# Block sums of weights in a two-layer diffusion kernel: from VectorE to accumulating loads, with turned signs in the activations

## The chip, the core and the metric

The kernel runs on one core of a Trainium2 chip. The core has a matmul engine (TensorE, PE in the profile, with its weight loads as PEld), VectorE (DVE), ScalarE (ACT), GpSimd (POOL) and SyncE (SP); the last one only issues transfers here. Transfers run on 16 DMA engines that all issuing engines share. The metric is the device time of one execution in microseconds (us); lower is better. The median of three runs of the kernel before is 872.34 us (872.25 to 872.8).

## The reference

One sequence of 512 latent tokens and 256 context tokens of width 1024 goes through two layers, and a normalisation ends it. Layer 0 is a retention mixer, layer 1 a gated MLP that mixes tokens in chunks of 128. The change lies in layer 1:

```python
def gmlp_chunk_mixer(h, w_in, vnorm_g, w_s, b_s, w_out):
    u = h @ w_in[:, :GM_WIDTH]                       # GM_WIDTH = 2048
    v = (h @ w_in[:, GM_WIDTH:2 * GM_WIDTH]).astype(F32)
    z = h @ w_in[:, 2 * GM_WIDTH:]
    v = v - jnp.mean(v, axis=-1, keepdims=True)
    v = v * lax.rsqrt(jnp.mean(v * v, axis=-1, keepdims=True) + NORM_EPS) * vnorm_g.astype(F32)
    ...
    mixed = jnp.einsum('gij,bnjgc->bnigc', w_s.astype(F32), vg) + b_s.astype(F32).T[:, :, None]
    y = u * mixed.reshape(b, l, w).astype(u.dtype)
    return (y * jax.nn.silu(z)) @ w_out
```

All of it is float32.

## The kernel before

**Seven products instead of eight.** A projection h @ w is cut into 2 x 2 blocks: token halves and feature halves of h, row halves and column halves of w. A "quad" is four weight blocks 11, 12, 21, 22 of 512 KB each (two transfers of 256 KB). Instead of eight block products the kernel computes seven, in the way of Strassen and Winograd, from sums of weight blocks and sums of activation blocks. The table `USES` names the weights' side: B11, B21 and B22 are plain blocks, T1 = 12 - 11, T2 = 22 - T1, T3 = 22 - 12, T4 = 21 - T2. `WITH` names the activations' side: A11, A12, A22 plain, S1 to S4 sums. The products are added up in PSUM banks and, through a `snap` (a copy of a bank) and a `plus` (bank and snap combined), into the four output blocks.

**Split operands.** Each float32 operand is cut into a high and a low part in the fast float32 format (`split`, line 133: ScalarE casts the high part, shown as CAST hl<-raw; VectorE subtracts, shown as TENSOR_TENSOR hl<-raw,hl), and each product is three matmuls (`mm3`). A product of a quad is 24 matmuls of 256 columns.

**The stream of weights.** One object, `Stream`, holds the order of all products (`items`) and of all loads (`loads`). `get` hands the next product its split weights and splits two products ahead (`upto`), into four `hl` buffers. `pump` issues the next load from SyncE as soon as one of the raw slots is free (for layer 1's u/z quads and the output projection: seven slots of 512 KB, w0 to w6); a slot comes free when the last product that needs its block is split (`drop`). `sum` forms T1 to T4 on VectorE in place in the raw slots (shown as TENSOR_TENSOR raw<-raw): T1 into 11's slot, T2 into the same, T3 into 12's, T4 into 21's.

**Layer 1.** First come four quads of v (`v1`, products in pairs, `PAIRED`), whose results are spilled to HBM as vt by GpSimd; then eight quads of u and z (`("u", i)`, products in the order `SINGLE` = B11, T1, T2, B21, T3, B22, T4), each with one block row of u and one of z; beside each quad the chunk mixing (`spatial`, `norm_vt`, `gate_f`). After quads 2, 4 and 6 a quarter of the output projection follows (`out1`, quarter 2 in two halves around quad 7), and the last quarter at the end. The operands A11 to S4 of layer 1 are made once, by `half_sum`, `first_half` and `second_half`, and serve both the v quads and the u/z quads.

**What sets the order.** Instructions of TensorE, ScalarE, VectorE and SyncE go through one helper (`Queue`), so the profile shows them all at its line 54 and is read by tile names; GpSimd's transfers show at the line that issues them (142 for spills, 1400 for the residual). Each engine runs its own instructions in order. A scheduler places them from the text, with orders pinned for TensorE, ScalarE and VectorE in places; transfers of SyncE and of GpSimd are issued in the order that the scheduler gives, each after its waits, and a transfer that waits holds up all behind it on the same issuing engine. The output projection already has eight accumulating loads from GpSimd (o<-x, the residual).

Of the kernel before, what the change touches and what calls it, by code (L numbers as in the profile page):

```python
# [67 lines left out]
def hybrid_kernel(ctx, tc, xT_d, cT_d, cv_d, sv_d, rows_d, ada0_d, adag_d, w_d, rope_d, dec_d, ws_d, id_d, out_d):  # L68
# [83 lines left out]
    PAIRED = ("B11", "B21", "T1", "T2", "B22", "T3", "T4")  # L152
    SINGLE = ("B11", "T1", "T2", "B21", "T3", "B22", "T4")

    class Stream:
# [18 lines left out]

        def load(self, key, slots, stage, parts):
            self.loads.append((key, slots, stage, parts))

# [4 lines left out]
        def pump(self):  # L182
            while self.sent < (self.cap or len(self.loads)):
                key, slots, stage, parts = self.loads[self.sent]
                ok = [s for s in self.free if s in slots]
                if stage > self.stage or not ok:
                    return
                self.free.remove(ok[0])
                r = st([P, 1024], ok[0], name="raw")
                for dst, src in parts:  # L190
                    load(dst(r), src)
                self.raws[key] = r
                self.left[key] = [ok[0], sum(it[0] == key[0] and key[1] in it[2] for it in self.items)]
                self.sent += 1

        def upto(self, n, late=None):

            while self.done < min(n, self.limit or len(self.items)):
# [24 lines left out]
        def sum(self, n):  # L223
# [3 lines left out]
            q, name, uses, at, place = self.items[n]  # L227
            if name[0] not in ("T", "gated") or any((q, u) not in self.raws for u in uses):
                return
# [7 lines left out]
            else:  # L237
                dve.tensor_tensor(r, raw(uses[0]), raw(uses[1]), ALU.subtract)

# [89 lines left out]
    A = {}  # L329
# [44 lines left out]
    class Product:  # L374

        def __init__(self, product, done, side=None, z="tm"):
            self.product, self.done, self.side, self.z_tag, self.s = product, done, side, z, {}

        def snap(self, key, bank):
            t = self.s[key] = t2("snap")
            act.copy(t, bank)

        def plus(self, key, bank, name):
            t = self.s.pop(key)
            dve.tensor_tensor(t, bank, t, ALU.add)
            self.done(name, t)
# [479 lines left out]
    def background():  # L868
        for i in range(4):
# [324 lines left out]
    def half_sum(hf, m):  # L1194
        if hf == 1:
# [65 lines left out]
    def second_half():  # L1261
# [362 lines left out]
```

## Time and profile before

| | |
|---|---|
| median of three runs | 872.34 us |
| profiled execution | 872.05 us, span 870.0 us |
| TensorE busy | 860.7 us, 99% |
| VectorE busy | 713.8 us, 82% |
| ScalarE busy | 457.8 us, 53% |
| GpSimd busy | 58.4 us, 7% |
| moved by DMA | 153.81 MB, mean 177 GB/s |

The span is the time from the first to the last instruction; the profiled execution's own time is 2.05 us longer. A group of the profile reads: engine, operation, output<-input, shape, count, then busy time in us and the mean of one in ns, then the idle time of that engine before these instructions, with what ended most of it. In the 40 slices of the span each digit is a busy share in tenths. A DMA queue's row gives packets, megabytes and the time its packets took as a share of 16 engines; q1 is SyncE's queue, q0 GpSimd's. A row of the windows gives the stretch, its length, each engine's busy time with the number of instructions, and last the granted TensorE clock, the DMA share and GB/s.

### The profile page before, as it was taken

The page shows a single profiled execution, that of the slowest core. Times are in us where ns is not written, and L with a number is a line of the kernel's source. Part 1 is how long each engine was busy: PE and PEld are TensorE (multiplying, and loading weights), DVE is VectorE, ACT ScalarE, POOL GpSimd, SP SyncE. Part 2 cuts the span into 40 slices and gives each one's busy share as a digit, 9 for nine tenths or more (in the row PEclk, how much of TensorE's full clock was granted, in tenths as well). Part 3 has the DMA queues.
Part 4 walks back from the last instruction along what each step waited for, and adds up shares of the span by engine and source line. Part 5 has one row for each costly group of instructions (what it writes and reads, how often), then busy time and mean ns, then how long its engine had stood idle before and what let it go on. Part 6 is the DMA issues. An engine that isn't in the chain of part 4 may idle for free.

```text
span 870.0 us, 17009 instructions
## 1 busy us (share of the span) xinstructions
PE 860.7 (99%) x6906; PEld 824.3 (95%) x6906; DVE 713.8 (82%) x998; ACT 457.8 (53%) x709; POOL 58.4 (7%) x96
## 2 busy tenths in 40 slices
PE   8999999999999999999999999999999999999997
PEld 7899999999999999999989899999999899899986
DVE  4799978699789777888677679999899488688995
ACT  4475644434545346637363549744666456256434
POOL 0001201102102011000000002011000000000110
PEclk9999999999999999999999999999999999999999
DMA  9943967557667458747164602535435036035523
GB/s 349 406 155 105 310 220 262 162 186 234 203 226 244 144 195 324 267 159 249 67 213 151 198 21 108 198 133 206 135 122 194 25 122 201 18 122 170 122 41 105
DMA packets 75774, 153.81 MB, mean 177 GB/s; under 512 B 7728, under 2 KB 34864, under 8 KB 75696
## 3 DMA queue, kind: packets, MB, share of 16 engines
q1 hardware_dynamic: 67392, 128.40, 44.1%
q0 software_dynamic: 7872, 24.12, 8.1%
q8 instruction: 54, 0.88, 0.4%
q10 hardware_dynamic: 432, 0.20, 0.1%
q14 instruction: 24, 0.20, 0.1%
HBM read 128.58 MB, written 24.12 MB: 176 GB/s over the span
## 4 chain that ended last, share of the span: by engine, by line
PE 96%; DMA 2%; ACT 0%; DVE 0%; SPq 0%; issue 0%; DVEq 0%; ACTq 0%
PE pst L54 96%; DMA raw<-in_w_dram 1%; DMA ada_w<-in_ada_dram 1%; DVE o L54 0%; ACT junk L54 0%; SPq L54 0%; ACT fss L54 0%; ACT o L54 0%; DVE fss L54 0%; ACT hl L54 0%; DVEq L1620 0%; ACTq L54 0%
## 5 line engine op out<-in xcount | busy, mean ns | idle before, releaser
L54 DVE TENSOR_TENSOR hl<-raw,hl 128x1024 fp32r<-128x1024 f32 (+2 forms) x197 | 234.8, 1197 | 69.1 <-ACT hl L54 68.8
L54 ACT CAST hl<-raw 128x1024 fp32r<-128x1024 f32 (+2 forms) x197 | 203.0, 1034 | 138.2 <-PE pst L54 57.6
L54 PE MATMUL pst<-hl,oS 128*128 128x256 f32 x1152 | 133.2, 276 | 0.0
L54 PE MATMUL pst<-oS,hl 128*128 128x256 f32 x1104 | 132.6, 277 | 0.1
L54 PEld LDWEIGHTS pst<-hl,oS 128*128 128x128 f32 x1152 | 131.8, 188 | 0.4 <-issue 0.4
L54 PEld LDWEIGHTS pst<-oS,hl 128*128 128x128 f32 x1104 | 128.2, 188 | 1.0 <-ACT oS L54 0.6
L54 PE MATMUL pst<-oA,hl 128*128 128x256 f32 x936 | 116.6, 279 | 0.9 <-DVE hl L54 0.5
L54 PEld LDWEIGHTS pst<-oA,hl 128*128 128x128 f32 x936 | 110.6, 188 | 3.2 <-ACT hl L54 1.0
L54 DVE TENSOR_TENSOR raw<-raw 128x1024 f32<-128x1024 f32 x92 | 111.9, 1218 | 0.8
L54 ACT COPY snap<-pst 128x512 f32<-128x512 f32 x92 | 53.6, 584 | 90.5 <-PE pst L54 90.4
L54 PE MATMUL pst<-hl,oA 128*128 128x256 f32 x768 | 92.7, 277 | 0.0
L54 PE MATMUL pst<-og,hl 128*128 128x256 f32 x768 | 91.1, 278 | 0.0
L54 PEld LDWEIGHTS pst<-hl,oA 128*128 128x128 f32 x768 | 89.5, 188 | 0.2
L54 PEld LDWEIGHTS pst<-og,hl 128*128 128x128 f32 x768 | 89.2, 188 | 0.3
L54 PE MATMUL pst<-v,ph 128*128 128x512 f32 x192 | 59.8, 393 | 0.0
L54 PE MATMUL pst<-hl,ya 128*128 128x512 f32 (+1 forms) x246 | 59.1, 386 | 0.0
L54 PEld LDWEIGHTS pst<-hl,ya 128*128 128x128 f32 x246 | 45.3, 188 | 9.5
L54 DVE TENSOR_TENSOR snap<-pst,snap 128x512 f32<-128x512 f32 x69 | 47.1, 683 | 5.1 <-PE pst L54 5.1
L54 PE MATMUL pst<-hl,hc 128*128 128x256 f32 x384 | 46.1, 276 | 0.0
L54 PEld LDWEIGHTS pst<-hl,hc 128*128 128x128 f32 x384 | 44.7, 188 | 0.0
L54 ACT CAST ph<-pf 128x512 fp32r<-128x512 f32 x24 | 14.8, 618 | 55.3 <-DVE pf L54 54.8
L54 PEld LDWEIGHTS pst<-v,ph 128*128 128x128 f32 x192 | 36.1, 188 | 7.1
(186 smaller groups left out, 1022.7 us busy)
## 6 DMA issues: line engine op xcount, KB each, us to landing
raw<-in_w_dram SPq DMA_DIRECT2D x224, 256.0 KB, 4.0
bg<-in_adag_dram SPq DMA_DIRECT2D x32, 512.0 KB, 4.2
ada_w<-in_ada_dram SPq DMA_DIRECT2D x16, 512.0 KB, 9.0
raw<-in_w_dram SPq DMA_DIRECT2D x16, 512.0 KB, 4.4
bg<-in_dec_dram SPq DMA_DIRECT2D x12, 512.0 KB, 4.3
v<-snap POOLq DMA_DIRECT2D x16, 256.0 KB, 5.6
z<-snap POOLq DMA_DIRECT2D x16, 256.0 KB, 5.0
v<-v SPq DMA_DIRECT2D x8, 512.0 KB, 4.3
```

What stands on the lines that cost most here:

```text
L54: made = op(*args, **kw)
```

## The change

The u/z quads no longer have their sums formed on VectorE. The signs of the recipe are turned so that all weight sums are plain additions: with T1 = 11 + 12, T2 = 22 + 12 + 11 and T3 = 22 + 12, a tile can be loaded with one block, and the others are added to it in SBUF by accumulating loads that GpSimd issues (`accum_op=ALU.add`). The table `SUMMED` says which. Six tiles are loaded for a quad in place of four. T4 is T2's tile with block 21 added on top after T2 has been split, so T2's slot stays taken until T4 is split. Per quad that is 12 plain transfers of 256 KB in place of 8, and 10 accumulating ones; over eight quads 32 and 80 more. The v quads keep VectorE's sums, with T1 now an addition.

The turned signs are put into the activations, once for both sets of quads: S1, S2 and S4 come from differences where there were sums (and the reverse), S2 with a scale of -1 in its split; and in `Product`, with `turned`, the snaps of T1 and T2 are taken with a scale of -1 and `plus` subtracts the bank.

```diff
+    SUMMED = {"B11": ("11",), "T1": ("11", "12"), "T2": ("22", "12", "11"), "B21": ("21",), "T3": ("22", "12"), "B22": ("22",)}
...
+        def loaded(self, q, slots, stage):
+
+            for name in SINGLE:
+                if name == "T4":
+                    self.items.append((q, name, ("T2",), "T2", None))
+                    continue
+                self.items.append((q, name, (name,), name, None))
+                first, *more = SUMMED[name]
+                self.load((q, name), slots, stage, parts_of(q, first), [parts_of(q, u) for u in more])
+
+        def add(self, r, parts):
+            for dst, src in parts:
+                nc.gpsimd.dma_start(dst(r), src, accum_op=ALU.add)
...
                 for dst, src in parts:
                     load(dst(r), src)
+                for p in more:
+                    self.add(r, p)
...
                 split((hl[:, 0, :], hl[:, 1, :]), r, late)
+                if q[0] == "u" and name == "T2":
+                    self.add(r, parts_of(q, "21"))
...
-            if n >= len(self.items) or n in self.summed:
+            if q[0] == "u" or name[0] not in ("T", "gated") or any((q, u) not in self.raws for u in uses):
                 return
...
-                dve.tensor_tensor(r, raw(uses[0]), raw(uses[1]), ALU.subtract)
+                dve.tensor_tensor(r, raw(uses[0]), raw(uses[1]), ALU.add if q[0] == "v1" else ALU.subtract)
...
-        Q.quad(("u", i), SINGLE)
-        for u in RAWS:
-            Q.load((("u", i), u), W, 2, parts_of(("u", i), u))
+        Q.loaded(("u", i), W, 2)
...
+            if self.turned and key != "s1":
+                act.activation(t, bank, AF.Copy, scale=-1.0)
+            else:
+                act.copy(t, bank)
...
+            if self.turned and key != "s1":
+                dve.tensor_tensor(t, t, bank, ALU.subtract)
+            else:
+                dve.tensor_tensor(t, bank, t, ALU.add)
...
-                dve.tensor_tensor(shs, sh1[:, 0:4], sh1[:, 4:8], ALU.add)
+                dve.tensor_tensor(shs, sh1[:, 4:8], sh1[:, 0:4], ALU.subtract)
...
-                dve.scalar_tensor_tensor(v, acc[:, m, sl], gs1[:, m:m + 1], v, ALU.mult, ALU.add)
+                dve.scalar_tensor_tensor(v, acc[:, m, sl], gs1[:, m:m + 1], v, ALU.mult, ALU.subtract)
...
-            dve.scalar_tensor_tensor(v[:, k, :], v[:, k, :], shs[:, k:k + 1], f11[:, k, :], ALU.add, ALU.subtract)
+            dve.scalar_tensor_tensor(v[:, k, :], v[:, k, :], shs[:, k:k + 1], f11[:, k, :], ALU.add, ALU.add)
         op("S2")
-        keep("S2", v)
+        h, l = (A["S2"][:, i].rearrange("p k t -> p (k t)") for i in range(2))
+        vf = v.rearrange("p k t -> p (k t)")
+        act.activation(h, vf, AF.Copy, scale=-1.0)
+        dve.scalar_tensor_tensor(l, vf, -1.0, f32(h), ALU.mult, ALU.subtract)
         yield
-        dve.tensor_tensor(f12, f12, v, ALU.subtract)
+        dve.tensor_tensor(f12, v, f12, ALU.subtract)
...
-        prods = {q: Product(tokens, v1_done(q), z="ps") for q in (a, b)}
+        prods = {q: Product(tokens, v1_done(q), z="ps", turned=True) for q in (a, b)}
...
-        prod = Product(features, got.__setitem__)
+        prod = Product(features, got.__setitem__, turned=True)
```

Where the accumulating loads stand on GpSimd, between quads 1 and 2 (raw_7625 is T3 of quad 1, raw_7490 T2 of quad 1, raw_7726 T1, raw_7781 T2 and raw_7880 T3 of quad 2; a row with x2 is the two halves of one block):

```order
L191 DMA raw_7625<-in_w_dram 128x512 x2
L191 DMA raw_7726<-in_w_dram 128x512 x2
L191 DMA raw_7781<-in_w_dram 128x512 x2
L191 DMA raw_7490<-in_w_dram 128x512 x2
L191 DMA raw_7781<-in_w_dram 128x512 x2
L191 DMA raw_7880<-in_w_dram 128x512 x2
L191 DMA raw_7781<-in_w_dram 128x512 x2
```

The fourth row makes T4 of quad 1 out of its T2 tile, and stands behind T1 and the first round of T2 of quad 2; the last makes T4 of quad 2. Before, GpSimd had nothing at this place, as the end of its list shows (o<-x are the residual's loads):

```order
 L142 DMA vt_6138<-snap 128x512
+L191 DMA raw<-in_w_dram 128x512 x3
 L142 DMA vt_6140<-snap 128x512
-L1400 DMA o_7528<-x_6142 128x512
-L1400 DMA o_7529<-x_6144 128x512
-L1400 DMA o_7530<-x_6146 128x512
-L1400 DMA o_7531<-x_6148 128x512
```

Between the last spill of vt and the residual's loads stood nothing; now 65 accumulating loads stand there.

On VectorE, quad 1's last products and the start of quad 2, before (raw_7603 is quad 1's block 21, which becomes T4; raw_7309 its T2; hl are the low halves of splits):

```order
L54 TENSOR_TENSOR hl_7812<-raw_7603,hl_7812 128x1024
L54 TENSOR_TENSOR ya_7532<-ya_7744,ya_7532 128x512
L54 TENSOR_TENSOR raw_7603<-raw_7603,raw_7309 128x1024
L54 TENSOR_TENSOR hl_7843<-raw_7344,hl_7843 128x1024
L54 TENSOR_TENSOR hl_7889<-raw_7347,hl_7889 128x1024
```

and the same place now (raw_7592 is the tile of B21, raw_7625 of T3, raw_7663 of B22):

```order
L54 TENSOR_TENSOR hl_7844<-raw_7592,hl_7844 128x1024
L54 TENSOR_TENSOR ya_7550<-ya_7768,ya_7550 128x512
L54 TENSOR_TENSOR hl_7877<-raw_7625,hl_7877 128x1024
L54 TENSOR_TENSOR hl_7925<-raw_7663,hl_7925 128x1024
```

The sum that made T4 is gone from the place, and nothing took its turn.

More of the change, by code (lines that the diff above doesn't have):

```diff
@@ L173, in single, with load @@
             self.items.append((q, name, ("w",), "w", None))
-        def load(self, key, slots, stage, parts):
-            self.loads.append((key, slots, stage, parts))
+        def load(self, key, slots, stage, parts, more=()):
+            self.loads.append((key, slots, stage, parts, more))
+        def loaded(self, q, slots, stage):
[9 more added lines that the diff above has]
+                nc.gpsimd.dma_start(dst(r), src, accum_op=ALU.add)
         def pump_n(self, n):
@@ L183, in pump @@
             while self.sent < (self.cap or len(self.loads)):
-                key, slots, stage, parts = self.loads[self.sent]
+                key, slots, stage, parts, more = self.loads[self.sent]
                 ok = [s for s in self.free if s in slots]
@@ L227, in sum @@
             q, name, uses, at, place = self.items[n]
-            if name[0] not in ("T", "gated") or any((q, u) not in self.raws for u in uses):
+            if q[0] == "u" or name[0] not in ("T", "gated") or any((q, u) not in self.raws for u in uses):
                 return
@@ L374, in hybrid_kernel, with __init__ @@
     class Product:
-        def __init__(self, product, done, side=None, z="tm"):
-            self.product, self.done, self.side, self.z_tag, self.s = product, done, side, z, {}
+        def __init__(self, product, done, side=None, z="tm", turned=False):
+            self.product, self.done, self.side, self.z_tag, self.turned, self.s = product, done, side, z, turned, {}
         def snap(self, key, bank):
             t = self.s[key] = t2("snap")
-            act.copy(t, bank)
+            if self.turned and key != "s1":
+                act.activation(t, bank, AF.Copy, scale=-1.0)
+            else:
+                act.copy(t, bank)
         def plus(self, key, bank, name):
             t = self.s.pop(key)
-            dve.tensor_tensor(t, bank, t, ALU.add)
+            if self.turned and key != "s1":
+                dve.tensor_tensor(t, t, bank, ALU.subtract)
+            else:
+                dve.tensor_tensor(t, bank, t, ALU.add)
             self.done(name, t)
```

## Prediction, made before the changed kernel was run

> **What bounds the kernel now.** I read the page first, then the waits of TensorE, then the order of time around layer 1, then the DMA queues there. The page:
>
> ```profile
> span 870.0 us, 17009 instructions
> PE 860.7 (99%) x6906; PEld 824.3 (95%) x6906; DVE 713.8 (82%) x998; ACT 457.8 (53%) x709; POOL 58.4 (7%) x96
> PE   8999999999999999999999999999999999999997
> DMA  9943967557667458747164602535435036035523
> PE 96%; DMA 2%; ACT 0%; DVE 0%; SPq 0%; issue 0%; DVEq 0%; ACTq 0%
> L54 ACT CAST hl<-raw 128x1024 fp32r<-128x1024 f32 (+2 forms) x197 | 203.0, 1034 | 138.2 <-PE pst L54 57.6
> L54 DVE TENSOR_TENSOR hl<-raw,hl 128x1024 fp32r<-128x1024 f32 (+2 forms) x197 | 234.8, 1197 | 69.1 <-ACT hl L54 68.8
> L54 DVE TENSOR_TENSOR raw<-raw 128x1024 f32<-128x1024 f32 x92 | 111.9, 1218 | 0.8
> L54 ACT COPY snap<-pst 128x512 f32<-128x512 f32 x92 | 53.6, 584 | 90.5 <-PE pst L54 90.4
> ```
>
> TensorE is busy 99% of the span and carries 96% of the chain that ended last. VectorE at 82% is not the bound. The weight sums are the third group (raw<-raw, 1218 ns each). All that TensorE waited for a named releaser, in the whole execution, is this:
>
> ```profile
> PE pst L54 <- DMA ident<-in_id_dram: 1.2, 1, 1.2
> PE pst L54 <- DVE eps L54: 1.1, 1, 1.1
> PE pst L54 <- DVE hl L54: 0.5, 1, 0.5
> PE pst L54 <- ACT hl L54: 0.4, 1, 0.4
> ```
>
> One of these 3.2 us belongs to VectorE's splits, and the constants named in the first two show that they lie at the start. In layer 1 the matmuls follow each other without a hole (start, duration):
>
> ```profile
> 626.74 5.70 PE L54 MATMUL pst<-oA,hl 128*128 128x256 f32 x48
> 647.61 5.70 PE L54 MATMUL pst<-oA,hl 128*128 128x256 f32 x48
> 668.48 2.98 PE L54 MATMUL pst<-oA,hl 128*128 128x256 f32 x24
> 671.30 22.14 PE L54 MATMUL pst<-hl,ya 128*128 128x512 f32 x96
> 828.09 2.98 PE L54 MATMUL pst<-oA,hl 128*128 128x256 f32 x24
> ```
>
> The first two rows are T4 of u/z quad 0 and of quad 1, each together with the first product of the next quad; the third is T4 of quad 2, the fourth the output projection after it, the last T4 of quad 7. A quad takes 647.61 - 626.74 = 20.87 us of TensorE. So the time saved on VectorE has nowhere to appear; the question is only whether the new transfers can starve TensorE.
>
> **The change, part by part.**
>
> *VectorE.* 8 quads x 4 sums x 1.218 = 39 us leave VectorE. TensorE waits for none of them (rows above), so this is worth 0.
>
> *Prices of the new transfers.* The kernel before has accumulating loads already, eight of 256 KB in the output projection. Here is the window 790 to 830, where four of them and 14.5 plain transfers of that size are the traffic, and 835 to 850 with the other four; then two of them on GpSimd:
>
> ```profile
> q1 hardware_dynamic: 1944, 3.79, 28.0%
> q0 software_dynamic: 576, 1.05, 15.8%
> raw<-in_w_dram SPq DMA_DIRECT2D x12, 256.0 KB, 3.5
> o<-x POOLq DMA_DIRECT2D x4, 256.0 KB, 4.0
> ```
>
> ```profile
> q0 software_dynamic: 576, 1.05, 46.1%
> ```
>
> ```profile
> 809.46 0.85 POOL L1400 DMA_DIRECT2D o<-x  x1 [0.67 <-DVE o L54]
> ```
>
> A plain 256 KB load occupies all 16 DMA engines for 0.28 x 40 x 0.262/3.79 = 0.774 us. An accumulating one occupies them for 0.158 x 40/4 = 1.58 us, in the second window 0.461 x 15/4 = 1.73 us: twice a plain load. It lands 4.0 us after its issue and holds GpSimd for 0.85 us.
>
> *Traffic of a quad.* Before: 8 loads and one 512 KB vt (1.55 us by size) = 7.7 us in 20.87. After: 6 tiles instead of 4, so 12 loads, and 10 accumulating loads (T1 2, T2 4, T3 2, T4 2): 9.3 + 15.8 + 1.55 = 26.6 us. A quad now needs more DMA time than TensorE time. From 671.30 to 828.09 (156.8 us) lie five quads, 133 us, with six further 512 KB output tiles (9.3) and four old accumulations (6.3): 148.6 us, 95% of it. That fits, since the two output projections of 22 us in it ask for little and seven slots hold work ahead. Quads 0, 1 and 2 follow one another with no projection between.
>
> *The tight place: T4 of quad 1.* Its tile is T2's tile with one more block added, and the add may be issued only after T2's split, on GpSimd's in-order queue behind T1 and the first round of T2 of quad 2. Ahead of it on the DMA engines, from the time that quad 1's T1 tile has landed: 16 accumulating loads (quad 1: 2 + 4 + 2; quad 0's T4: 2; quad 2: T1 2, T2 2; its own 2), 20 plain loads (8 of quad 1, 12 of quad 2, which share the engines), one vt: 16 x 1.58 + 20 x 0.774 + 1.55 = 42.3 us. The start follows from the slot that quad 0's first tile leaves:
>
> ```profile
> 600.36 1.05 ACT L54 CAST hl<-raw 128x1024 fp32r<-128x1024 f32 x1 [1.62 <-PE pst L54]
> ```
>
> 600.36 + 1.05 + 1.20 (the low half) + 3.5 (landing) = 606.1; 606.1 + 42.3 = 648.4. TensorE wants T4 at 647.61, and cast and low half take 2.25 before, so the tile must be there by 645.4; with some 0.4 for the completion, an estimate out of the 4.0 - 1.58 that a landing takes besides its transfer, by 645.0. It is 3.4 us late. The second round of T2 waits for the first to land; two adds back to back cover 3.16 of the 4.0 us, so the engines idle 0.84 us there unless loads fill it: 4.2 us. I take that as T4 of quad 1.
>
> *Other T4s.* Quad 0's has only its own quad's adds ahead, and the same sum leaves it about on time; quads 3, 5 and 7 have 8 us of spare DMA time between them. Bounds 0 and 5 us together; I take 1.6, nearer the low end because 95% still fits.
>
> *The TensorE clock after a wait.* How a wait acts on the granted clock shows at the end:
>
> ```profile
> 864.00:868.00 4.00, 0.09 (x1) 0.00 (x0) 1.97 (x7) 1.75 (x5) 0.00 (x0) 1.00 0.60 223
> 868.00:870.00 2.00, 0.00 (x0) 0.00 (x0) 0.00 (x0) 0.00 (x0) 0.00 (x0) 0.53 0.26 100
> ```
>
> With next to no matmuls (0.09 us) the clock, the third number from the end, stays at 1.00 for 4 us, then drops to 0.53. My wait of 4.2 us stands at that edge: 0, or up to 2 us if the next 4 us run at half; I take 0 by the first row. The Trainium skill (TensorE: Matmul & The Clock Gate, The HAM clock gate) puts the drop after about 3.4 us of idleness; by that the wait would add some 1.7 us. The row, at 4 us, is later than the page, so the sum goes by the row.
>
> *GpSimd and SyncE.* 80 adds x 0.85 = 68 us of issue in the 201 us between the first and the last T4 row, so GpSimd is not full; each add waits for its load or for the round before, and what is queued behind it is other adds and, early on, the last spills of vt, which are read only for quads 4 to 7. SyncE issues 32 more loads, each when a slot comes free; the slot is counted in the start time above. Cost beside the 4.2 us: 0; without the spare issue time, 0.85 us for each add that stands ahead of a late one.
>
> *ScalarE, VectorE forms.* The snaps become a scaled activation. The nearest row is
>
> ```profile
> L54 ACT ACTIVATE junk<-pst 128x512 f32<-128x512 f32 x30 | 17.8, 596 | 9.0 <-PE pst L54 8.9
> ```
>
> against 584 ns for the copy: 24 x 12 ns on an engine that is 53% busy. The subtraction in `plus` and the turned S2 have the same sizes as before. Each is hidden behind the matmuls of the next product (2.8 us); without that cover 0.3 us. A late cast of T4 does hold ScalarE's queue: the casts of the next quad's first products stand behind it, and VectorE's bank sums too, so TensorE does not win the wait back, but loses little more, because a split takes 2.25 us and a product 671.30 - 668.48 = 2.8 us.
>
> *Sum.* The profiled execution took 872.05 us (span 870.0 and 2.05 around it), 0.29 under the median of 872.34. 872.05 + 4.2 + 1.6 = 877.9; on the median 878.1. I say 878.
>
> **The rivals.** *Hidden, no change: 872.3.* If packets of two queues overlap better than alone, the prices are the best half microseconds of this trace:
>
> ```profile
> 4.50:10.00 5.50, 4.34 (x44) 3.22 (x44) 1.85 (x5) 2.98 (x7) 0.00 (x0) 1.00 1.07 394
> 810.50:811.00 0.50, 0.50 (x7) 0.50 (x6) 0.50 (x2) 0.50 (x1) 0.00 (x0) 1.00 1.06 193
> ```
>
> Plain traffic at 394 GB/s is 0.67 us per load, accumulating at 193 GB/s 1.36 us: 16 x 1.36 + 20 x 0.67 + 1.34 = 36.5, done at 642.6, 2.4 us early. The deciding point is a price of some 1.4 us for an add beside cheap loads. This is the case that ends on the other side, not slower. The Trainium skill (DMA: Bandwidth & Descriptors, Anatomy of one DMA) gives 2.0 us plus bytes at 436 GB/s for any DMA from GpSimd, which would make an add 2.6 us to landing and 0.6 us of the engines, and no T4 late; the row of 4.0 us and 15.8% for four speaks against it,.
>
> *DMA-bound throughout: about 891.* At 1.73 us an add, quads cost 28.1: 140.6 + 9.3 + 6.9 = 156.8 of 156.8 us, no spare at all. If the adds' waits for landings leave the engines idle a tenth of the time, T4 of each pair of quads is late: 15.7 us, and T4 of quad 1 by 16 x 0.15 = 2.4 us more than 4.2. 872.3 + 15.7 + 6.6 = 894.6 with all of it, about 891 with three quarters of the stage loss. For it: the second window; against it: the window with plain traffic beside has the cheaper adds.
>
> *The sums held TensorE after all: faster.* Only the 0.5 us that TensorE waited for VectorE could shrink, which gives 871.8; a gain over 1.7 us would need a wait that the trace doesn't show.
>
> **How the numbers follow.** T4 late in the first three quads, 878: 0.46. Hidden: 0.27. DMA-bound throughout: 0.23. Faster: 0.04. A difference of 0.2%, 1.7 us, is about what a measurement of this kernel can tell from none. That gives faster 0.04, same 0.27, slower 0.69. The range starts at 872, inside the hidden case, and goes to 893, which leaves about 0.15 below and 0.06 above. The likeliest case alone spans 875 to 884.
>
> **What would show it.** Right: in the profile after, TensorE's idle time sits at a few places, the longest before the oA,hl product near 648, released by a split whose cast waited for the accumulating load; DMA share near full from 606 to 650; raw<-raw of VectorE down to 60; accumulating raw<-in_w_dram x80 near 4 to 8 us to landing; q0 about 1.6 us of the engines per 256 KB. The hidden case would show no TensorE wait beyond the start and q0 under 1.45. The DMA-bound case would show waits at T4 of quads 3, 5 and 7 too, and a DMA share near 10 tenths there. Wrong altogether would be a wait named for VectorE, ScalarE or GpSimd's own issue in place of the landing, or idle time in the stage of v1.

## The result, and the profile after

The changed kernel takes 897.04 us (median of 4 runs, 894.52 to 898.75) against 872.34 (872.25 to 872.8) in the same session: 1.028 times as long, 95% interval 1.0255 to 1.0305. The forecast was 878.0 with a range of 872 to 893, so the direction held and the size did not: 24.7 us were lost where 5.8 were forecast. The profiled execution is the fastest of the four, 894.52 us with a span of 892.7, which is 22.7 over the span of before.

The page of the changed kernel, in the order of the rows shown of before (spans, engines, DMA in slices, the chain, three groups, the adding loads' issues):

```profile
span 892.7 us, 17229 instructions
PE 868.1 (97%) x6906; PEld 829.4 (93%) x6906; DVE 676.7 (76%) x966; ACT 458.0 (51%) x709; POOL 127.3 (14%) x176
DMA  9943957567667387565273415769998898899723
PE 77%; DMA 11%; DVE 5%; issue 3%; ACT 2%; POOL 1%; SPq 0%; DVEq 0%; POOLq 0%; ACTq 0%
L191 POOL DMA_DIRECT2D raw<-in_w_dram x80 | 69.2, 1021 | 184.3 <-DMA raw<-in_w_dram 122.4
L54 DVE TENSOR_TENSOR raw<-raw 128x1024 f32<-128x1024 f32 x60 | 72.9, 1218 | 0.4
raw<-in_w_dram POOLq DMA_DIRECT2D x80, 256.0 KB, 6.4
```

VectorE gave up its 32 sums (x92 to x60) and TensorE gained nothing from that. DMA now stands in the chain with 11% where it had 2%, and the last third of the DMA slices is full, where before it stood near 4 tenths. The groups by line say what GpSimd did: of its idle time, 122 us went to waiting for a landing, that is for the load or for the round before. What TensorE waited for, by releaser (us in total, times, longest), and its own rows from the stage of u and z (start, duration; in brackets the wait ahead):

```profile
PE pst L54 <- DVE snap L54: 10.6, 4, 7.1
PE pst L54 <- ACT snap L54: 3.5, 3, 1.6
PE pst L54 <- DVE hl L54: 1.3, 1, 1.3
```

```profile
634.42 8.15 PE L54 MATMUL pst<-oA,hl 128*128 128x256 f32 x48 [7.12 <-DVE snap L54]
...
658.24 5.90 PE L54 MATMUL pst<-oA,hl 128*128 128x256 f32 x48
...
683.44 22.56 PE L54 MATMUL pst<-hl,ya 128*128 128x512 f32 x96
...
734.97 3.01 PE L54 MATMUL pst<-oS,hl 128*128 128x256 f32 x24 [1.55 <-ACT snap L54]
...
792.24 5.72 PE L54 MATMUL pst<-oA,hl 128*128 128x256 f32 x48 [1.26 <-DVE snap L54]
...
802.15 3.09 PE L54 MATMUL pst<-oS,hl 128*128 128x256 f32 x24 [1.46 <-ACT snap L54]
...
844.33 2.32 PE L54 MATMUL pst<-oS,hl 128*128 128x256 f32 x18 [1.32 <-DVE hl L54]
...
850.81 3.00 PE L54 MATMUL pst<-oA,hl 128*128 128x256 f32 x24 [1.67 <-DVE snap L54]
```

The first is T4 of quad 0, which starts 7.7 us later than before; the second is T4 of quad 1, 10.6 later and with no wait of its own; the third is the output projection after quad 2, 12.1 later. So TensorE had lost 12.1 us by the end of quad 2 (0.3 of them before the u/z quads), and lost the other 10.6 from there on. In quads 3 to 7 the five waits shown, of 1.3 to 1.7 us at T2, T4 and B22, and one of 0.5 at T4 of quad 3 make 7.8 us; the rest goes at the restarts and in slower products.

### The profile page after: what moved, and what is told of

The parts are those of the page before. It is cut to its first block, busy times and chain, and to the rows that moved or that the text cites. A ratio compares the mean times of both kernels' runs of the same rounds, so it can differ in the third digit from the quotient of the medians.

```text
span 892.7 us, 17229 instructions
## 1 busy us (share of the span) xinstructions
PE 868.1 (97%) x6906; PEld 829.4 (93%) x6906; DVE 676.7 (76%) x966; ACT 458.0 (51%) x709; POOL 127.3 (14%) x176
## 4 chain that ended last, share of the span: by engine, by line
PE 77%; DMA 11%; DVE 5%; issue 3%; ACT 2%; POOL 1%; SPq 0%; DVEq 0%; POOLq 0%; ACTq 0%
PE pst L54 77%; DMA raw<-in_w_dram 7%; DVE hl L54 3%; DMA vt<-vt 2%; DMA ada_w<-in_ada_dram 1%; DVE snap L54 1%; DMA xq<-in_xT_dram 1%; ACT hl L54 1%; POOL raw L191 1%; DVE raw L54 1%; DVE bns L54 1%; DMA cv<-in_cv_dram 0%; DVE o L54 0%; SPq L54 0%; ACT vt L54 0%
## 5 line engine op out<-in xcount | busy, mean ns | idle before, releaser
L54 PE MATMUL pst<-oS,hl 128*128 128x256 f32 x1104 | 134.9, 279 | 4.9 <-ACT snap L54 3.5
L54 PE MATMUL pst<-oA,hl 128*128 128x256 f32 x936 | 120.0, 284 | 10.7 <-DVE snap L54 10.6
L54 PEld LDWEIGHTS pst<-oA,hl 128*128 128x128 f32 x936 | 113.8, 192 | 13.5 <-DVE snap L54 11.3
L191 POOL DMA_DIRECT2D raw<-in_w_dram x80 | 69.2, 1021 | 184.3 <-DMA raw<-in_w_dram 122.4
L54 ACT COPY snap<-pst 128x512 f32<-128x512 f32 x68 | 39.6, 585 | 76.2 <-PE pst L54 76.1
L54 DVE TENSOR_TENSOR raw<-raw 128x1024 f32<-128x1024 f32 x60 | 72.9, 1218 | 0.4
```

The costliest lines, as they stand in the source:

```text
L54: made = op(*args, **kw)
L191: nc.gpsimd.dma_start(dst(r), src, accum_op=ALU.add)
```

## How T4 of quad 0 came 7.7 us late

Three things stand behind that one wait. First the landing. GpSimd's list between quads 0 and 1 (raw_6959 is quad 0's T2 tile, which becomes T4; raw_7490 is T2 of quad 1; raw_7625 its T3):

```order
L191 DMA raw_7490<-in_w_dram 128x512
L191 DMA raw_6959<-in_w_dram 128x512
L191 DMA raw_7490<-in_w_dram 128x512
L142 DMA vt6_6140<-snap_7521 128x512
L191 DMA raw_7490<-in_w_dram 128x512
L191 DMA raw_6959<-in_w_dram 128x512
L191 DMA raw_7490<-in_w_dram 128x512
L191 DMA raw_7625<-in_w_dram 128x512 x2
```

The second half of T4's block stands behind the second round of quad 1's T2, which has to wait until the first round has landed. In time, on GpSimd:

```profile
613.62 2.91 POOL L191 DMA_DIRECT2D raw<-in_w_dram  x3
621.73 1.71 POOL L191 DMA_DIRECT2D raw<-in_w_dram  x2 [4.62 <-DMA raw<-in_w_dram]
```

The three of 613.62 are issued, the next two only at 621.73. T4's half is the second of these by the list, and lands when ScalarE's cast can start, 7 us on; in the windows of 5 us from 615 to 630 the DMA share is 1.04, 1.08 and 1.13, so the engines were full (a packet counts whole in the window where it starts, so a full stretch can read somewhat over 1):

```profile
629.74 2.94 ACT L54 CAST hl<-raw 128x1024 fp32r<-128x1024 f32 x3 [11.77 <-DMA raw<-in_w_dram]
```

Second, VectorE's list. TensorE had been idle from 627.30 (634.42 - 7.12). VectorE's rows:

```profile
630.81 1.23 DVE L54 TENSOR_TENSOR hl<-raw,hl 128x1024 fp32r<-128x1024 f32 x1 [12.48 <-ACT hl L54]
631.96 0.68 DVE L54 TENSOR_TENSOR snap<-pst,snap 128x512 f32<-128x512 f32 x1
632.56 1.22 DVE L54 TENSOR_TENSOR hl<-raw,hl 128x1024 fp32r<-128x1024 f32 x1
633.69 0.68 DVE L54 TENSOR_TENSOR snap<-snap,pst 128x512 f32<-128x512 f32 x1
```

The low half of T4 is done at 632.04, but the product starts at 634.42, just after the second bank sum ends (634.37). VectorE had stood idle for 12.5 us at the late split; the two bank sums, which TensorE needs, stand behind it in VectorE's list and, with another low half between them, take 2.4 us more. So 4.7 us of the wait go until T4 has landed and is split, and 2.4 to the queue behind it.

Third, the clock. Windows of the changed kernel (the third number from the end is the granted clock):

```profile
630.00:632.00 2.00, 0.00 (x0) 0.00 (x0) 1.19 (x2) 2.00 (x3) 0.00 (x0) 1.00 1.02 181
632.00:634.00 2.00, 0.00 (x0) 0.00 (x0) 2.00 (x4) 1.96 (x2) 0.00 (x0) 0.64 0.61 169
634.00:636.00 2.00, 1.57 (x7) 1.58 (x8) 2.00 (x3) 1.35 (x2) 0.00 (x0) 0.50 0.85 270
638.00:640.00 2.00, 2.00 (x13) 2.00 (x13) 1.26 (x3) 0.17 (x1) 1.04 (x2) 0.65 0.96 186
```

A mean of 0.64 over 632 to 634 puts the fall from 1.00 to 0.50 at 632.6, 5.3 us after the last matmul; 0.65 over 638 to 640 puts the return at 639.4. The row of 48 matmuls took 8.15 us instead of 5.70: 2.45 us more. With 7.12 and 2.45 and the 0.45 of a small wait, 10.0 of the 12.1 us are named. Of the other 2.1, 0.3 were lost before the u/z quads, and most of the rest are products that ran slower until about 706 (10.17 us from 670.36 to 680.53, where before it was 9.89) at a granted clock of 1.00. Twenty-four matmuls of 256 columns at 648.07 take 2.99 us where before, at 637.72, they took 2.88, and the projection's 96 of 512 columns take 22.56 instead of 22.14: 4.6 and 4.4 ns for each matmul, whatever its length. Such rows come back behind later waits (3.01 at 734.97, 3.09 at 802.15); the runs give no cause.

## The experiments

The kernel before took 872.1 to 872.9 us (medians) on the chips of these runs; ratios are to it. The theories: *engines* (an adding load takes twice the time of the 16 engines, and the stage asks for nearly all they have), *order* (GpSimd's list puts T4's block behind rounds that wait), *landings and slots* (a tile holds one of seven slots through two or three landings), *forms* (the turned signs).

### Which part of the change: the signs, the loads, and how many

The turned signs alone, the sums back on VectorE:

```diff
-        Q.loaded(("u", i), W, 2)
+        Q.quad(("u", i), SINGLE)
+        for u in RAWS:
+            Q.load((("u", i), u), W, 2, parts_of(("u", i), u))
```

> The turned signs, the scaled snaps and the subtracting plus stay; the u/z sums go back to VectorE, four tiles a quad, no adding loads in those quads. Theory 'the loads' (all 24.7 us come from the 80 adding and 32 further plain loads): 872.3, at most 0.5 off, and no T4 waits. Theory 'the forms' (the scaled snaps or the turned S2 hold ScalarE at the places where TensorE waits for a snap): 875 to 880.

872.12 us, ratio 1.0001 (0.9991 to 1.001). The signs and the scaled snaps cost nothing; the loss is the loads'.

Adding loads for T1 and T3 only:

```diff
-    SUMMED = {"B11": ("11",), "T1": ("11", "12"), "T2": ("22", "12", "11"), "B21": ("21",), "T3": ("22", "12"), "B22": ("22",)}
+    SUMMED = {"B11": ("11",), "T1": ("11", "12"), "T3": ("22", "12"), "B21": ("21",), "B22": ("22",)}
+    VSUM = {"T2": ("T3", "B11"), "T4": ("B21", "B11")}
```

> Only T1 and T3 are made by adding loads (five tiles and four adds a quad); T2 (T3's tile plus block 11) and T4 (block 21 plus T2) are formed on VectorE. A quad asks for 10 x 0.78 + 4 x 1.55 + 1.55 = 15.6 us of the DMA engines in 20.87. Theory 'capacity': 872 to 874. Theory 'chains' (each landing of an adding load comes too late for its product, whatever the load): the waits of T2 and T1 stay, 880 or more.

873.07 us, ratio 1.0019 (1.0008 to 1.0031): four adds and five tiles a quad are hidden but for 0.9 us at T4 of quad 7. Half of VectorE's sums of these quads are gone here, and nothing is won by it.

### The price or the order

Plain transfers in the adding loads' places:

```diff
-                nc.gpsimd.dma_start(dst(r), src, accum_op=ALU.add)
+                nc.gpsimd.dma_start(dst(r), src)
```

> The 80 transfers from GpSimd stay at their places, with the same waits, bytes and issue, but they copy instead of adding (so the weight sums of layer 1's u and z are left out: a tile holds its last block only). The queue's transfers then cost about 0.78 us of the 16 engines instead of 1.55. Theory 'capacity' (the engines are 93% full because an add costs twice a load): a quad asks for 12 x 0.78 + 10 x 0.78 + 1.55 = 18.7 us in 20.87, transfers land 3 to 4 us after issue, and the time falls to 872 to 877. Theory 'order' (GpSimd's list puts T4's block behind rounds that wait for landings, whatever these cost): still late at T4 of quad 0, 885 or more.

877.64 us, ratio 1.0074 (1.005 to 1.0097). Some 19 of the 24.7 us are gone when the same transfers in the same order copy instead of adding; 5.5 stay, most of them in one place. From the page and TensorE's rows of this run:

```profile
q0 software_dynamic: 14272, 45.10, 15.8%
629.46 7.21 PE L54 MATMUL pst<-oA,hl 128*128 128x256 f32 x48 [2.88 <-DVE snap L54]
```

GpSimd's queue takes 0.158 x 875.5 = 138 us of the engines here, 0.219 x 892.7 = 195.5 in the changed kernel: an add costs 57/80 = 0.71 us more than a copy. T4 of quad 0 is still late, by 2.9 us, and its row takes 7.21 instead of 5.70; the only other wait in the u/z quads is 0.77 us at T2 of quad 2.

The order alone, with the adding loads at their price; GpSimd's list is pinned:

```diff
+    adds = Queue(tc, nc.gpsimd)
+    adds.kept = True
...
-                for p in more:
-                    self.add(r, p)
+                self.waiting += [(r, p) for p in more]
...
+                for rp in self.ripe:
+                    self.add(*rp)
+                self.ripe, self.waiting = self.waiting, []
```

> The adds keep their number and price; GpSimd's list is held to one order in which T4's block of a quad goes ahead of the next quad's T1 and T2 blocks, and blocks for a tile are queued one split later. Theory 'order': the wait of 7.1 us at T4 of quad 0 goes with the half clock behind it, 897 - 7 - 2.5, and T4 of later quads win too: 880 to 887. Theory 'capacity': the same transfers are asked for, so what T4 wins, T1 and T2 of the next quads lose: 893 to 900, with TensorE's waits at other products.

902.77 us, ratio 1.0357 (1.0342 to 1.0373). T4 of quad 0 starts at 626.92 without a wait, so the order was what made it late; but all of it and more is lost at T2 of quads 1, 2, 4 and 6. These four waits, and a window of the first of them:

```profile
PE pst L54 <- ACT snap L54: 20.4, 4, 7.1
638.00:640.00 2.00, 0.00 (x0) 0.00 (x0) 1.90 (x5) 0.49 (x2) 1.39 (x3) 1.00 0.05 10
```

Here the engines stand idle in the middle of the worst stretch (DMA share 0.05): GpSimd's first place in the list waits for a split, and six adds go out at once behind it. This order is therefore no fair test of "the best order"; it shows that the order decides which product waits.

Both together:

```diff
-                adds.dma_start(dst(r), src, accum_op=ALU.add)
+                adds.dma_start(dst(r), src)
```

> The 80 transfers from GpSimd are plain (the block sums of layer 1's u and z are left out, a tile holds its last block) and GpSimd's list is held to the order in which T4's block goes ahead of the next quad's. Two causes together: with the price at 0.78 us and the order put right nothing is left, 872 to 873. If the 5.5 us left with plain transfers are not the order's but the transfers' number or their chains, 876 to 878 again.

874.12 us (872.54 to 875.27), ratio 1.002 (1.0009 to 1.0031); in the profiled execution, 872.58 and so one of the fastest, TensorE waits nowhere in layer 1 by more than 0.4 us. With copies the order is worth some 3.5 us, with adds it cost some 6. From 600 to 650 the engines are nearly as full as in the changed kernel (0.96 there) and TensorE is without a hole; later they are less full (0.51 to 0.79 in the next four stretches of 50 us, against 0.83 to 0.95):

```profile
600.00:650.00 50.00, 50.00 (x443) 50.00 (x442) 36.42 (x54) 30.24 (x43) 15.26 (x29) 1.00 0.90 308
```

Fewer, larger adds, and plain transfers in small pieces:

```diff
-            for dst, src in parts:
-                nc.gpsimd.dma_start(dst(r), src, accum_op=ALU.add)
+            nc.gpsimd.dma_start(r.rearrange("p (s n) -> p s n", s=2), parts, accum_op=ALU.add)
```

> The same sums by adding loads, each block as one transfer of 512 KB in place of two of 256 KB: 40 issues on GpSimd instead of 80, the same bytes added. Theory 'capacity': the engines are asked for the same time, 10 x 1.55 a quad, so 895 to 900. Theory 'issue and landing' (each issue's 0.85 us and each landing's fixed part stand on the path): 40 issues and as many fixed parts fewer, 880 to 890.

902.1 us, ratio 1.0346 (1.0293 to 1.0398): half the issues win nothing; whether they lose the 5 us more is not certain, since the changed kernel's interval reaches 1.0305. A 512 KB add lands 8.5 us after its issue (median), and GpSimd's list is another one (T4's block of quad 0 stands ahead of quad 1's T2), so the run does not price the issues alone.

```diff
-                adds.dma_start(dst(r), src)
+                adds.dma_start(dst(r).rearrange("p (x n) -> p x n", x=4), src)
...
+        comb = lambda b: w_d[b].rearrange("p (x k n) -> p x k n", x=4, k=2)[:, :, kh, :]
```

> Like the run with plain transfers in the mended order, but each of the 80 transfers reads and writes pieces of 512 B in place of rows of 2 KB (same bytes; the block sums of layer 1's u and z are left out, and other columns of the weights are read). Nothing is added in SBUF; the pieces are to make the transfers dear. Their price is not known: if 256 KB in pieces take 1.3 to 1.6 us of the engines, theory 'engine time' says as late as adding loads in that order, 885 to 903; at 0.8 to 1.0 it says 872 to 876. Theory 'the adding itself' (a wait that only accumulation has) says 872 to 875 at any price.

875.02 us, ratio 1.0026 (1.0014 to 1.0037), but the pieces were not dear: GpSimd's queue took 16.3% of 873.1 us, 5.6 us more than with whole rows, 0.07 us a transfer. Both theories allow that time; the run tells nothing between them. That adding costs only through its engine time was therefore not shown with a copy of the same price.

### Where in the program

Adding loads in quads 0 to 2 only, and (with LOADED = 3 to 7) in the others only:

```diff
+    LOADED = (0, 1, 2)
...
-        Q.loaded(("u", i), W, 2)
+        if i in LOADED:
+            Q.loaded(("u", i), W, 2)
+        else:
+            Q.quad(("u", i), SINGLE)
```

> Adding loads in quads 0, 1 and 2 only; the five later quads have VectorE's sums and four tiles. In the changed kernel TensorE stood 12.1 us behind at the output projection after quad 2. Theory 'capacity, stage by stage': 872.1 + 12.1 = 884, give or take 1. Theory 'the later quads' demand reaches back' (loads ahead for quads 3 and 4 share the engines): 1 to 4 us less than that.

885.66 us, ratio 1.0157 (1.0128 to 1.0187): +13.3.

> Adding loads in quads 3 to 7 only; quads 0 to 2 have VectorE's sums and four tiles. Theory 'capacity, stage by stage': the whole change cost 24.7 us and quads 0 to 2 alone 13.3, so 872.3 + 11.4 = 883.7, give or take 1.5. Theory 'carried on' (the later waits come from the disorder that quads 0 to 2 leave behind): 872 to 876.

883.97 us, ratio 1.0135 (1.0099 to 1.0172): +11.6. The two make 24.9 against 24.7: the loss is made stage by stage and is not carried on. The traces agree: with quads 0 to 2 alone TensorE falls no further behind after quad 2.

In every second quad (LOADED = 1, 3, 5, 7), and in three of these:

> Adding loads in every second quad only (1, 3, 5 and 7). Such a quad asks for 12 x 0.78 + 10 x 1.54 + 1.55 = 26.3 us of the engines, its neighbour for 8 x 0.78 + 1.55 = 7.8, together 34.1 in 41.7 us of TensorE. Theory 'capacity over a stage' (seven slots carry work from the lean quad to the full one): 872 to 875. Theory 'capacity of each quad' (slots and the order of the adds let no work be done ahead): half of the loss, 880 to 885.

881.92 us, ratio 1.0112 (1.0082 to 1.0141). "Capacity over a stage" would have given 872 to 875 and falls; the next run shows where it does not.

> Adding loads in quads 1, 3 and 5 only. With quad 7 as well it took 881.9, and of the profiled 10.9 us 3.3 were lost before the output projection ahead of quad 7. Theory 'the place of quad 7' (half output projections around it, the residual's adding loads in the same list): 875 to 876.5. If the loss is spread over all quads that have adding loads: 879 to 880.

876.78 us, ratio 1.0042 (1.0023 to 1.0062): quads 1, 3 and 5 cost 3.9 us together, and quad 7 costs 5 to 6 more. In the profile of this run the one wait in the u/z quads is at T2 of quad 1, with half a clock behind it:

```profile
638.55 4.62 PE L54 MATMUL pst<-oS,hl 128*128 128x256 f32 x24 [2.86 <-ACT snap L54]
```

Quads 3 and 5, each right behind an output projection and ahead of a lean quad, lost nothing in either profile. For them "capacity over a stage" holds; it fails for quad 1, which has no projection ahead of it, and for quad 7. The windows of the run with quad 7 show its place, the half output projection ahead of it and the quad:

```profile
800.00:805.00 5.00, 5.00 (x34) 4.50 (x33) 3.94 (x8) 1.70 (x4) 0.00 (x0) 1.00 1.10 271
805.00:810.00 5.00, 5.00 (x23) 4.09 (x22) 4.47 (x7) 0.67 (x2) 2.53 (x3) 1.00 1.05 386
815.00:820.00 5.00, 3.94 (x35) 3.74 (x33) 3.54 (x4) 4.41 (x6) 0.86 (x2) 1.00 0.39 57
830.00:835.00 5.00, 2.30 (x11) 2.31 (x12) 4.72 (x5) 1.70 (x2) 0.00 (x0) 0.76 0.39 142
```

The engines are full (1.10 and 1.05) while the projection's weights come in beside the quad's adds, then stand half idle while TensorE waits. That all slots are taken by then, so that nothing can be asked for ahead, is a reading and was not tried. The mean over the stretch says nothing of either. The same kernel without the residual's eight adding loads:

```diff
-            nc.gpsimd.dma_start(s, x1_d[2 * t + hf], accum_op=ALU.add)
```

> Adding loads in quads 1, 3, 5 and 7, and the residual's eight adding loads in the output projection left out (so the residual is missing from the output). Theory 'the residual's adds stand in the way' (in GpSimd's list and on the engines, four of them between 809 and 823): the 5 us of quad 7 go, 876 to 878. Theory 'quad 7's own tiles' (its loads wait for slots behind the output projection's weights): 880 to 882.

878.77 us (877.79 to 883.73), ratio 1.0085 (1.0054 to 1.0116), against 1.0112 (1.0082 to 1.0141) with them: the intervals overlap. In the two profiles TensorE loses 7.6 us in quad 7 with the residual's adds and 3.9 without; with one execution each, that half of quad 7's loss is the residual's is likely and not shown. Up to quad 7 GpSimd has the same list in both, and yet T2 of quad 1 waits 4.55 us in this profile and 1.24 in the other: one execution is no measure of a single wait.

### Fewer adds, and fewer or more slots

T4 back on VectorE (eight adds a quad), and T3 and T4 on VectorE (six):

```diff
-                    self.items.append((q, name, ("T2",), "T2", None))
+                    self.items.append((q, name, ("B21", "T2"), "B21", None))
```

> T1, T2 and T3 by adding loads as in the changed kernel; T4 is formed on VectorE from block 21 and T2's tile, so two of ten adds of a quad go, and T4 no longer depends on GpSimd's list. A quad asks for 12 x 0.78 + 8 x 1.54 + 1.55 = 23.2 us of the engines in 20.87. Theory 'capacity': quads 0 to 2 ask for 7 us more than they have, in place of 16, two quads and an output projection for 48.7 in 64; 875 to 880. Theory 'T4 alone' (all is lost by T4's late add and what it sets off): 872 to 873.

885.07 us (882.29 and 887.85), ratio 1.015 (1.0075 to 1.0226): both forecasts missed, about half of the loss stays without any T4 in GpSimd's list. The longest wait is 4.5 us at T2 of quad 1.

```diff
+    SUMMED = {"B11": ("11",), "T1": ("11", "12"), "T2": ("22", "12", "11"), "B21": ("21",), "12": ("12",), "B22": ("22",)}
+    VSUM = {"T3": ("12", "B22"), "T4": ("B21", "T2")}
```

> T1 and T2 by adding loads, T3 (22 plus 12) and T4 (21 plus T2's tile) on VectorE: twelve loads and six adds a quad, 12 x 0.78 + 6 x 1.54 + 1.55 = 20.2 us of the engines in 20.87, full to 97%. Between four adds (873.1) and eight (885.1). Theory 'capacity decides where the sum passes 20.87': 872.5 to 875. Theory 'near full is full' (landings grow late before the engines are full): 876 to 882.

885.72 us (882.61 to 888.83), ratio 1.0155 (1.007 to 1.024): above both forecasts, and as far as two executions can tell not less than with eight. The group of VectorE's sums shows a new wait, 19.9 us for blocks that had not landed:

```profile
L54 DVE TENSOR_TENSOR raw<-raw 128x1024 f32<-128x1024 f32 x76 | 92.6, 1220 | 25.2 <-DMA raw<-in_w_dram 19.9
```

So 97% by the count of engine time is not free, where 75% (four adds) is; where between them the loss begins, this run can't say, since it also holds two more tiles in slots until their sums.

Six slots, eight slots (for which two of eleven snap buffers are given up), and six slots with plain transfers in the pinned order:

```diff
-        Q.loaded(("u", i), W, 2)
+        Q.loaded(("u", i), W[:6], 2)
```

> The changed kernel with six raw slots instead of seven for the u/z quads. Theory 'engines' (the 16 DMA engines' time is what the quads wait for): the same is asked for, 895 to 901. Theory 'slots times landing' (a tile holds its slot from issue through its landings to its split, and six tiles of a quad go through them in turn): a seventh of the slots less, quads 0 to 2 of 24.9 us each grow by up to 4, later ones less: 905 to 925.

911.81 us, ratio 1.0449 (1.0418 to 1.0479): 14 to 15 us for one slot, with the other order of GpSimd's list that comes with it. "Engines" alone would have left it at 897.

```diff
-    T2 = 11
+    T2 = 9
...
-        Q.loaded(("u", i), W, 2)
+        Q.loaded(("u", i), W + ["w8"], 2)
```

> The changed kernel with eight raw slots for the u/z quads; the room comes from nine snap buffers in place of eleven. Theory 'engines': 893 to 899. Theory 'slots times landing': 880 to 888. Over 900 would mean that the missing snap buffers hold something up, and the run would say nothing.

900.69 us, ratio 1.0321 (1.0275 to 1.0368), no better than with seven. The control, the kernel before with nine snap buffers:

> The kernel before with nine snap buffers in place of eleven, nothing else. If the buffers matter little: 872 to 873.5, and then the eight slots' 900.7 shows that a slot more wins nothing. If they are needed: 876 or more, and the run with eight slots stays undecided.

872.24 us, ratio 1.0002 (0.9993 to 1.0012). The kernel before does not miss the two buffers; that the changed one doesn't either was not tried. But the eighth slot also gives GpSimd another list: both halves of T4's block of quad 0 now stand behind all four adds of quad 1's T2, where with seven slots its first half stands behind one, and T4 of quad 1 stands behind both rounds of quad 2's T2. The longest waits of the run are at these two places, 5.9 and 5.0 us. So what a slot wins at an equal order stays open.

> Plain transfers in the mended order (block sums of layer 1's u and z left out), six raw slots instead of seven. With seven it took 874.1. Theory 'slots times landing': the landings are 5 us instead of 6.5, but a slot less makes T2 and T1 late: 878 to 890. Theory 'engines' (about 18.7 us asked for in 20.87): 873 to 876.

879.88 us, ratio 1.0083 (1.0054 to 1.0112): 5 to 6 us for the slot even with cheap transfers, here with the same rule for the order. With seven slots and landings of 5.1 and 5.5 us (medians from 600 to 860) the six tiles a quad had come in time but for some 2 us; with six slots they do not.

## Why the prediction was wrong

*VectorE* held. 39 us of sums left it and TensorE gained none: the changed kernel is slower, and neither four adds a quad (873.07) nor signs alone (872.12) came out under 872.

*Prices of the new transfers* held. The queues of the changed kernel from 600 to 860:

```profile
q0 software_dynamic: 11712, 22.03, 48.1%
q1 hardware_dynamic: 17593, 33.86, 38.7%
```

0.481 x 260 = 125 us, less six spills at 0.78, over 74 new and 4 old adds is 1.54 us an add (1.58 predicted); a plain load is 0.387 x 260 x 0.262/33.86 = 0.779 (0.774 predicted). The Trainium skill (DMA: Bandwidth & Descriptors, Rules for kernel authors) says that an accumulating transfer reads its destination and writes it later; an add that costs 1.54 us where a copy from the same queue costs 0.71 less agrees with that, and no run here shows the reading by itself.

*Other T4s* (term: 0 to 5, taken 1.6) is the step that failed by most, in both of its parts. T4 of quad 0, put at "about on time", waited 7.12 us (below). From 683.44 to the end, with quads 3 to 7, another 10.6 us were lost, of which waits at T4 are 3.4; 4.3 are waits at T2 and B22, for which the prediction had no term. The ground for the small term, "That fits", was the error: 148.6 us of demand in 156.8, a mean over five quads and some two and a half projections. The mean hides that in the changed kernel the demand comes in heaps: in windows of 5 us the engines are full from 640 to 665 and again from 810 to 830 (shares of 1.05 to 1.11), and at 0.28 from 830 to 835. Over 50 us it is 0.83 to 0.95 in quads 3 to 7, and TensorE is short of its 50 us in every window of the changed kernel (before, it had 50.00 in each):

```profile
600.00:650.00 50.00, 42.88 (x354) 42.69 (x353) 27.50 (x42) 24.67 (x36) 20.62 (x26) 0.93 0.96 235
650.00:700.00 50.00, 49.55 (x352) 46.21 (x352) 31.92 (x43) 27.74 (x43) 10.90 (x13) 1.00 0.93 250
700.00:750.00 50.00, 47.93 (x390) 46.42 (x389) 27.46 (x33) 25.69 (x37) 12.93 (x16) 1.00 0.86 207
750.00:800.00 50.00, 48.73 (x331) 44.46 (x330) 28.03 (x37) 18.71 (x25) 13.65 (x16) 1.00 0.95 226
800.00:850.00 50.00, 46.36 (x351) 43.74 (x349) 35.02 (x44) 25.02 (x37) 11.89 (x14) 1.00 0.83 206
```

The ledger counted engine time and left out that a tile is made by a chain of landings, load, first add, second add, 5.4 us for a load and 6.5 for an add under this load (medians from 600 to 860) instead of the 3.5 and 4.1 of before, while it holds one of seven slots. That these landings and the slots matter beside the engines' time is shown by the runs with six slots; how the 10.6 us divide between the two is not. The rival "DMA-bound throughout" came near this mechanism and its size for these quads (15.7 us, or three quarters of it), and its sign came too: waits at T4 of quads 3, 5 and 7 (0.5, 1.3 and 1.7 us). It got 0.23, and took for it a price of 1.73 us, which was not needed.

*The tight place: T4 of quad 1* (4.2 us) was the wrong tile. T4 of quad 1 has no wait of its own, because T4 of quad 0 (said to be "about on time") had already pushed everything back by 10. The sum for quad 0 counted only its own quad's adds ahead; GpSimd's list had quad 1's T2 rounds between the halves, and one of them waits for a landing. The order was there to be read, and was read for quads 1 and 2 only. That the order made this wait, and not the price alone, is shown by the pinned order (adds at their full price and no wait at 626.92) and by the plain transfers (2.9 us of wait left in the same order at the lower price).

"*Loses little more*" behind a late cast measured 2.4 us, the two bank sums and a low half in VectorE's list after T4's own; the prediction's sum had no term for it.

*Clock* (0) measured 2.45 us: the wait was 7.1 instead of 4.2. But 4.2 would not have been safe either. With plain transfers TensorE was idle from 626.58 and the clock fell at 628.9, after 2.3 us; it came back at 632.3:

```profile
628.00:629.00 1.00, 0.00 (x0) 0.00 (x0) 1.00 (x2) 1.00 (x1) 0.00 (x0) 0.96 0.80 250
632.00:634.00 2.00, 2.00 (x17) 2.00 (x17) 1.90 (x4) 0.07 (x1) 1.09 (x2) 0.92 0.70 189
```

One row of 4 us at 1.00 was taken for a limit, and was one draw.

*GpSimd and SyncE* at 0 fell for GpSimd in part: what stood behind a waiting add was said to be "other adds" at no cost, and one of these adds was T4's. That issue time itself costs nothing is not contradicted: 40 issues instead of 80 were no faster, though each of those transfers also landed later. *ScalarE, VectorE forms* at 0 held (872.12).

Of what would show it right, the count of sums (60), the landing (6.4 us), the DMA share (0.96 from 600 to 650) and the price came as said; the place of the longest wait did not. The sign of being wrong altogether, a wait named for VectorE or ScalarE, is of no use here: all of TensorE's waits in layer 1 are named so, and behind the longest stands the cast's wait of 11.77 us for a landing.

## What to carry to other kernels

Work that leaves an engine which nobody waits for is worth nothing, and the resource that takes it over must be checked in the fullest 10 us, not in the mean over a stage: here 95% of the DMA engines' time "fitted", and the five quads lost 10 us. A tile that is made by transfers that wait for each other needs its landings added up, under load, and held against the slots that it keeps; and an in-order list of such transfers is to be read at every place where a late product's piece may stand behind another's wait. One idle stretch of observed clock is a sample and no threshold: a wait of more than 2 us should be priced with the half clock behind it.

## What the runs showed of the hardware

The granted clock fell 2.3, 3.2, 4.7 and 5.3 us after the last matmul (plain transfers at quad 0, the pinned order at quads 4 and 1, the changed kernel at quad 0), always to 0.50 (the pinned order's two below; the other two stand above), and came back 2.9 to 5.0 us after the restart; the row behind the wait took 1.5 to 2.45 us longer. With adding loads in quads 0 to 2 only it fell after 2.1 us, while a wait of 2.94 us with the 512 KB adds passed at 1.00. The half clock lasted 3.4 us with plain transfers (628.9 to 632.3), 6.8 in the changed kernel (632.6 to 639.4) and 10.2 with adding loads in quads 0 to 2 (629.0 to 639.2, from mean clocks of 0.74 over 628 to 630 and 0.70 over 638 to 640): one, two and three times the same length. The Trainium skill (TensorE: Matmul & The Clock Gate, The HAM clock gate) says that activity is judged in free-running windows of about 3.4 us: that the delay is not fixed and that the half clock comes in such lengths agree with it, a fall after 2.1 or 2.3 us is earlier than the one idle window that it asks for. The 3.4 us ahead of the fall at 628.9 still held 1.1 us of matmuls (to 626.58).

```profile
640.00:642.00 2.00, 0.00 (x0) 0.00 (x0) 1.52 (x2) 2.00 (x5) 2.00 (x5) 0.51 0.96 133
...
734.00:736.00 2.00, 0.00 (x0) 0.00 (x0) 1.92 (x3) 0.76 (x2) 1.30 (x2) 0.91 0.51 82
```

An adding load costs 1.54 us of the 16 engines per 256 KB beside other traffic, 0.71 more than the same transfer as a copy from the same queue; pieces of 512 B cost a copy only 0.07 us more than rows of 2 KB, but 0.75 instead of 0.55 us of issue on GpSimd:

```profile
L54 POOL DMA_DIRECT2D raw<-in_w_dram x80 | 59.6, 750 | 169.9 <-DMA raw<-in_w_dram 68.0
```

Open remain the matmuls that run some 4 ns slower at a granted clock of 1.00 behind several waits, the share of the residual's loads in quad 7's loss, how much an eighth slot wins at an equal order, whether an add costs by its engine time alone, and an order of GpSimd's list that would be best at the full price.
